# ScalarE instead of VectorE for the product of the first comparison with the large part of the gate

## The chip, the cores and the metric

The kernel runs on one core of one Trainium2 chip. The metric is the device time of one execution in microseconds; the figure before is the median of three runs. The engines are named as the profile names them: PE is TensorE, DVE is VectorE, ACT is ScalarE, POOL is GpSimd, SP issues the DMAs.

## The reference, cut to what matters

Two layers, each a mixer and a feed-forward block of retrieved experts (PEER), and then two more layers of another kind. The change lies in the feed-forward block of the first two layers alone. For each of 256 tokens and 8 heads it finds 16 experts out of 128 x 128, weighs them by a softmax and adds their outputs:

```
top_s, top_pos = lax.top_k(cand, PEER_TOPK)
eid = jnp.take_along_axis(cand_id, top_pos, axis=-1)
g = jax.nn.softmax(top_s, axis=-1)
ue = u_tab[eid]
ve = v_tab[eid]
act = jax.nn.gelu(jnp.einsum('pd,phkd->phk', xb, ue))
return jnp.einsum('phk,phkd->pd', g.astype(xb.dtype) * act, ve)
```

The expert number is i1 * 128 + i2. The kernel gathers nothing: it computes gelu(u . x) for all 16384 experts as a dense product, and makes a dense gate matrix with g where a token has chosen the expert and zero elsewhere.

## The kernel before, in words

`peer` (L764) works on 128 row blocks of 128 experts, in two phases. The **u phase** (L994 to L1013) is a loop over b, and each turn of it is called a body here. Body b issues, in this order:

1. `u_split(b + 2)`: the DMA of a block of the table, its rounded copy `hi` on ACT (L153) and the remainder `lo` on DVE (L81, in `tt`). So the two parts of block b are made two bodies ahead.
2. what the body before left in `later`.
3. a share of `tasks` (the top-16 search, in the first 54 bodies), or, in bodies 55 to 121, `group(b)`.
4. `u_block(b)`: 24 matmuls of block b into one bank `up` (L228 to L230), and the gelu on ACT: L971 in place for the P tokens whose gate already stands in row b, L974 into the row for the other tokens. The product of gate and gelu (DVE, `Wx<-up,Wx` or `Wy<-up,Wy`) goes to `later`.
5. what the body before left in `after`.

PE, DVE and ACT run this loop under `manual_schedule`, so each keeps the order in which the code issues its instructions.

A **group** makes the gate of 8 tokens for all experts. `g_onehots` compares a row of numbers with i2 (tile B) and with i1 (tile L), then multiplies L with the large half-precision part gH of the gate (tile A) and, in place, with the small part gL. Two bodies later `g_matmuls` makes 16 matmuls (L939), eight with A and then eight with L, into two banks `gg`, after the matmuls of that block. One body after that `g_store` puts the result away: DVE multiplies the rows whose gelu already stands there (`Wy<-gg,Wy`, `Wx<-gg,Wx`), ACT copies the rest (L952). There are 32 groups, in bodies 55, 56, 58, 60, 62, 64, 67, 69, 71, 73, 75, 78 and so on to 121: mostly every second body, and after every fifth or sixth group a distance of three bodies (67, 78, 89, 102 and 113 follow such a distance).

So the DVE order of a body with a group is lo(b+2), product of row b-1, B, L, A, L; the gg matmuls of group b come after block b+2, and its store is in body b+3.

The **v phase** (L1039 on) multiplies the finished rows with the second table. Before its sums can begin it needs the banks that the u phase held.

The other names: `i1T`, `i2T`, `gH`, `gL` are filled by `store` in `to_pairs` (L897 to L901), once for each half of the tokens.

Of the kernel before, what the change touches and what calls it, by code (L numbers as in the profile page):

```python
# [8 lines left out]
F32 = mybir.dt.float32  # L9
# [5 lines left out]
AF = mybir.ActivationFunctionType  # L15
ALU = mybir.AluOpType
# [4 lines left out]
S = 256  # L21
# [26 lines left out]
def kernel(ctx: ExitStack, tc: tile.TileContext, x, cols, ada_w, w_in, gm_wt, gm_vnorm, w_out,  # L48
# [3 lines left out]
    ve, se, pe, gp, sy = nc.vector, nc.scalar, nc.tensor, nc.gpsimd, nc.sync  # L52
# [24 lines left out]
    def two_banks(name):  # L77
        return psc["pool"].tile([128, 2, 512], F32, tag="c", name=name, bufs=2)

    def tt(out, a, b, op):  # L80
        return ve.tensor_tensor(out, a, b, op)  # L81

    def ts(out, a, s1, s2, op0, op1=None):
        if op1 is None:
            return ve.tensor_scalar(out, a, s1, None, op0)
        return ve.tensor_scalar(out, a, s1, s2, op0, op1)
# [452 lines left out]
    class Lead:  # L539
# [15 lines left out]
        def small(self, t, k0=0, k1=8):  # L555
            for k, wh, wl, g, d in self.parts(t):
                if k0 <= k < k1:
                    pe.matmul(d, lhsT=self.hT[1][:, k, t * 128:t * 128 + 128], rhs=wh[:, g * 512:g * 512 + 512],
                              start=False, stop=False, skip_group_check=True)
# [204 lines left out]
    def peer(l, hT, then):  # L764
        with ExitStack() as es:
            scr = es.enter_context(tc.tile_pool(name=f"pr{l}", bufs=1))
# [15 lines left out]
            i2T = scr.tile([128, S], F16, name="i2T")  # L782
            gH = scr.tile([128, S], F16, name="gH")
            gL = scr.tile([128, S], F16, name="gL")
            tasks = []
            tk = Scr(W, 20)
            st = {}
# [93 lines left out]
            def soft(t):  # L881
                s = st[t]
                e = s["e"]
                z = tk.tile([128, 8], F32, name="sm_z")
                ve.tensor_reduce(z, e, AX.X, ALU.add)
                ve.reciprocal(z, z)
                tt(e, e, z.rearrange("p (a b) -> p a b", b=1).to_broadcast([128, 8, 16]), ALU.mult)
                after.append(lambda: to_pairs(t))

            def to_pairs(t):  # L890
                s = st[t]
                ps = two_banks("tr")[:, 0, :]
                for n, src in enumerate((s["ii"][:, 0], s["ii"][:, 1], s["e"])):
                    pe.transpose(ps[:, n * 128:n * 128 + 128], src.rearrange("p a b -> p (a b)"), ident)
                c = slice(t * 128, t * 128 + 128)

                def store():  # L897
                    ve.tensor_copy(i1T[:, c], ps[:, 0:128])
                    ve.tensor_copy(i2T[:, c], ps[:, 128:256])
                    ts(gH[:, c], ps[:, 256:384], GSCALE, None, ALU.mult)  # L900
                    ve.scalar_tensor_tensor(gL[:, c], ps[:, 256:384], GSCALE, gH[:, c], ALU.mult, ALU.subtract)  # L901

                later.append(store)

# [13 lines left out]
            NG = 8  # L918

            def g_onehots(p0):  # L920

                shape = [128, NG // 2, 128, 2]
                A = scr.tile(shape, F16, name="A", tag="A", bufs=2)
                B = scr.tile(shape, F16, name="B", tag="B", bufs=2)
                L = scr.tile(shape, F16, name="L", tag="L", bufs=GL)
                it = iota2.rearrange("p (o i) q -> p o i q", o=1).to_broadcast(shape)
                tok = lambda a: a[:, p0:p0 + NG].rearrange("p (g o q) -> p g o q", o=1, q=2).to_broadcast(shape)
                tt(B, it, tok(i2T), ALU.is_equal)
                tt(L, it, tok(i1T), ALU.is_equal)
                tt(A, L, tok(gH), ALU.mult)  # L930
                tt(L, L, tok(gL), ALU.mult)
                return A, B, L

            def g_matmuls(p0, A, B, L):
                ps = two_banks("gg")
                for side in (A, L):
                    for n in range(NG):
                        a, q = divmod(n, 4)
                        pe.matmul(ps[:, a, q * 128:q * 128 + 128], lhsT=B[:, n // 2, :, n % 2], rhs=side[:, n // 2, :, n % 2],  # L939
                                  start=side is A and q == 0, stop=side is L, skip_group_check=True)  # L940
                return ps

            def g_store(p0, ps, nb):
                g3 = ps.rearrange("p g (q i) -> p (g q) i", q=4)
                for todo in (False, True):
                    for a, b0, b1 in ((Y, 0, NY), (W, NY, 128)):
                        wv, gv = a[:, :, p0:p0 + NG].rearrange("p i q -> p q i"), g3[:, :, b0:b1]
                        n = max(0, min(nb, b1) - b0)
                        if todo and n:
                            tt(wv[:, :, :n], gv[:, :, :n], wv[:, :, :n], ALU.mult)  # L950
                        if not todo and n < b1 - b0:
                            se.activation(wv[:, :, n:], gv[:, :, n:], AF.Copy)  # L952
# [4 lines left out]
            ready, after, later = [], [], []  # L957
# [18 lines left out]
            def group(b):  # L976
                p0 = st["groups"]
                st["groups"] += NG
                abl = g_onehots(p0)

                def matmuls():
                    banks = g_matmuls(p0, *abl)

                    def store():
                        g_store(p0, banks, st["block"])
                        st["stored"] += NG
                    later.append(store)
                after.append(lambda: after.append(matmuls))

            small_banks(True)  # L990
            for t in range(T):
# [2 lines left out]
            with tc.manual_schedule(engines={mybir.EngineType.PE, mybir.EngineType.DVE, mybir.EngineType.Activation}):  # L994
                for b in range(2):
                    u_split(b)
                for b in range(129):
                    st["block"] = b
                    u_split(b + 2)
                    now, later = later, []  # L1000
                    for f in now:
                        f()
                    if b == 128:
                        break
                    now, after = after, []
                    while tasks and spent < (b + 1) * total / TK:
                        spent += tasks[0][0]
                        tasks.pop(0)[1]()
                    if b > TK and st["groups"] < S and st["groups"] < (b + 1 - TK) * S / (GE - TK):
                        group(b)  # L1010
                    u_block(b)
                    for f in now:
                        f()  # L1013
# [616 lines left out]
    for l in range(2):  # L1630
        mixer(l, cur["hT"], then_norm(l, 4, "norm_ffn", 24, True))
        peer(l, cur["hT"], then_norm(1, 1, "norm_mix", 0, False, lambda: lead_half(w_in[1, :, 512:1024])) if l == 0 else then_even)
# [56 lines left out]
```

## Time and profile before

| what | us |
|---|---|
| median of three runs | 2326.93 (2321.4 to 2329.91) |
| the profiled execution, its own time | 2335.08 |
| its span | 2333.2 |
| PE busy | 2260.4 (97%) |
| DVE busy | 1762.8 (76%) |
| ACT busy | 1196.9 (51%) |
| granted TensorE clock, mean over the span | 0.993 |

A profile row of the timeline begins with the start in us from the start of the span and the duration in us. Durations overlap on one engine, since the next instruction starts before the last has written all of its result; what an instruction costs in a row of them is the distance from its start to the next start. The u phase with groups lies from 366 to 615 us in the first layer and from 1333 to 1582 us in the second.

### The profile page before, as it was taken

Reading aid. Unit: us, or ns where it says so; the run is one execution under the profiler, and the core shown is the slowest. Engines: PE = TensorE matmul, PEld = TensorE weight load, DVE = VectorE, ACT = ScalarE, POOL = GpSimd, SP = SyncE. Lnnn points to the kernel's source line nnn. Section 1 sums busy time; section 2 is a strip of 40 time slices with the busy share of each in tenths; the row PEclk is TensorE's granted clock in tenths of the full one; section 3 lists DMA queues with packets and bytes.
Section 4 is the critical chain, followed back from the end, with each engine's and each line's share of the span. In section 5 each row is a group of like instructions: output and inputs, shape, how many; then the busy total and the mean of one; then the engine's idle time right before and its main releaser. Section 6 shows DMA issues by size and latency. Waiting matters only on the chain.

```text
span 2333.2 us, 39116 instructions
## 1 busy us (share of the span) xinstructions
PE 2260.4 (97%) x14953; PEld 2021.3 (87%) x14953; DVE 1762.8 (76%) x3277; ACT 1196.9 (51%) x1925; POOL 13.3 (1%) x36
## 2 busy tenths in 40 slices
PE   5999999999999999999999999999999999999998
PEld 4889999999887787888899999998888877987796
DVE  7875999999867877666589899996555666577556
ACT  4645555554444444457455555544444554654454
POOL 0000000000000000000000000000000000000000
PEclk9999999999999999999999999999999999999999
DMA  8845555544568888644455554446656673443542
GB/s 321 280 139 159 185 181 172 156 153 154 172 207 286 299 298 278 210 140 127 138 158 186 183 158 153 157 142 196 190 187 187 203 226 97 133 136 116 173 153 82
DMA packets 122028, 424.11 MB, mean 182 GB/s; under 512 B 14433, under 2 KB 15841, under 8 KB 121842
## 3 DMA queue, kind: packets, MB, share of 16 engines
q1 hardware_dynamic: 121842, 421.63, 56.2%
q8 instruction: 117, 1.92, 0.3%
q14 instruction: 69, 0.57, 0.1%
HBM read 420.53 MB, written 1.05 MB: 181 GB/s over the span
## 4 chain that ended last, share of the span: by engine, by line
PE 78%; DVE 11%; DMA 6%; ACT 2%; issue 2%; SPq 0%; DVEq 0%; ACTq 0%
PE up L228 9%; PE up L229 8%; PE up L230 8%; PE op L1031 8%; PE op L1029 8%; PE op L1030 8%; DVE lo L81 4%; DMA Wx<-in_ada_w_dram 3%; PE pc L230 3%; PE pc L228 3%; PE pc L229 3%; DVE Wx L81 2%; PE gg L939 2%; DMA raw<-in_peer_v_dram 2%; PE op L238 2%
## 5 line engine op out<-in xcount | busy, mean ns | idle before, releaser
L81 DVE TENSOR_TENSOR lo<-raw,hi 128x1024 fp32r<-128x1024 f32 x686 | 835.4, 1222 | 323.1 <-ACT hi L153 322.2
L153 ACT ACTIVATE hi<-raw 128x1024 fp32r<-128x1024 f32 x686 | 720.0, 1052 | 266.6 <-PE pc L229 73.2
L230 PE MATMUL up<-hT_hi,lo 128*128 128x256 f32 x2048 | 581.7, 284 | 4.9 <-DVE lo L81 4.7
L228 PE MATMUL up<-hT_hi,hi 128*128 128x256 f32 x2048 | 585.8, 286 | 0.0
L229 PE MATMUL up<-hT_lo,hi 128*128 128x256 f32 x2048 | 580.0, 283 | 0.0
L230 PEld LDWEIGHTS up<-hT_hi,lo 128*128 128x128 f32 x2048 | 392.9, 192 | 8.4 <-DVE lo L81 8.4
L1031 PE MATMUL op<-hi,lo 128*128 128x512 f32 x976 | 388.3, 398 | 7.2 <-DVE lo L81 7.1
L229 PEld LDWEIGHTS up<-hT_lo,hi 128*128 128x128 f32 x2048 | 393.2, 192 | 0.0
L228 PEld LDWEIGHTS up<-hT_hi,hi 128*128 128x128 f32 x2048 | 392.9, 192 | 0.0
L1029 PE MATMUL op<-hi 128*128 128x512 f32 x976 | 387.9, 397 | 0.6 <-DVE Wx L81 0.5
L1030 PE MATMUL op<-lo,hi 128*128 128x512 f32 x976 | 387.2, 397 | 0.8 <-DVE lo L81 0.8
L1031 PEld LDWEIGHTS op<-hi,lo 128*128 128x128 f32 x976 | 184.2, 189 | 55.7 <-DVE lo L81 11.8
L1030 PEld LDWEIGHTS op<-lo,hi 128*128 128x128 f32 x976 | 184.1, 189 | 45.3 <-DVE lo L81 2.0
L1029 PEld LDWEIGHTS op<-hi 128*128 128x128 f32 x976 | 184.2, 189 | 44.7 <-DVE Wx L81 1.4
L228 PE MATMUL pc<-hT_hi,hi 128*128 128x256 f32 x568 | 161.1, 284 | 0.4 <-ACT hi L153 0.4
L229 PE MATMUL pc<-hT_lo,hi 128*128 128x256 f32 x568 | 160.9, 284 | 0.0
L230 PE MATMUL pc<-hT_hi,lo 128*128 128x256 f32 x568 | 160.7, 284 | 0.0
L971 ACT ACTIVATE up<-up 128x256 f32<-128x256 f32 (+31 forms) x140 | 37.7, 269 | 210.0 <-PE up L230 200.9
L153 ACT ACTIVATE hi<-Wy 128x256 fp32r<-128x256 f32 x120 | 50.1, 417 | 174.6 <-PE op L1030 174.6
L974 ACT ACTIVATE Wy<-up 128x256 f32<-128x256 f32 (+1 forms) x120 | 46.2, 385 | 166.2 <-PE up L230 166.0
L153 ACT ACTIVATE hi<-Wx 128x256 fp32r<-128x256 f32 x124 | 51.1, 414 | 126.5 <-PE op L1030 119.6
L228 PEld LDWEIGHTS pc<-hT_hi,hi 128*128 128x128 f32 x568 | 109.1, 192 | 1.4 <-ACT hi L153 1.3
(437 smaller groups left out, 3140.8 us busy)
## 6 DMA issues: line engine op xcount, KB each, us to landing
raw<-in_peer_ut_dram SPq DMA_DIRECT2D x256, 512.0 KB, 3.6
raw<-in_peer_v_dram SPq DMA_DIRECT2D x256, 512.0 KB, 4.3
Wx<-in_ada_w_dram SPq DMA_DIRECT2D x56, 512.0 KB, 5.6
raw<-in_even_w_dram SPq DMA_DIRECT2D x42, 512.0 KB, 3.6
raw<-in_w_in_dram SPq DMA_DIRECT2D x40, 512.0 KB, 4.8
raw<-in_peer_wq_dram SPq DMA_DIRECT2D x32, 512.0 KB, 4.1
raw<-in_odd_w_in_dram SPq DMA_DIRECT2D x32, 512.0 KB, 4.3
ada_raw<-in_ada_w_dram SPq DMA_DIRECT2D x30, 512.0 KB, 4.9
```

What stands on the lines that cost most here:

```text
L81: return ve.tensor_tensor(out, a, b, op)
L153: se.activation(hi, raw, AF.Copy)
L228: pe.matmul(dst, lhsT=wh[:, c0:c0 + 128], rhs=hh[:, k, :], start=first, stop=False, skip_group_check=True)
L229: pe.matmul(dst, lhsT=wh[:, c0:c0 + 128], rhs=hl[:, k, :], start=False, stop=False, skip_group_check=True)
L230: pe.matmul(dst, lhsT=wl[:, c0:c0 + 128], rhs=hh[:, k, :], start=False, stop=last, skip_group_check=True)
L238: pe.matmul(d, lhsT=a, rhs=wh[:, g * n:g * n + n], start=first, stop=False, **mk)
L939: pe.matmul(ps[:, a, q * 128:q * 128 + 128], lhsT=B[:, n // 2, :, n % 2], rhs=side[:, n // 2, :, n % 2], start=side is A and q == 0, stop= ...
L971: se.activation(ps[:, :P], ps[:, :P], AF.Gelu_apprx_tanh)
L974: se.activation(row(b)[:, P:], ps[:, P:256], AF.Gelu_apprx_tanh)
L1029: pe.matmul(d, lhsT=a, rhs=vh[:, s], start=first, stop=False, **mk)
L1030: pe.matmul(d, lhsT=a, rhs=vl[:, s], start=False, stop=False, **mk)
L1031: pe.matmul(d, lhsT=c, rhs=vh[:, s], start=False, stop=last, **mk)
```

## The change

DVE no longer makes A. In the body after the group, ACT makes it with eight `activation` copies, one for each token, each scaled by a per-partition number gF, which is a 32-bit copy of gH. The product with the small part overwrites L, so it has to wait for these eight; it moves to the end of that next body in DVE's order. The matmuls of the group stay where they were.

```
@@ peer
+            gF = scr.tile([128, S], F32, name="gF")
@@ to_pairs, store
+                    ve.tensor_copy(gF[:, c], gH[:, c])
@@ g_onehots
                 tt(B, it, tok(i2T), ALU.is_equal)
                 tt(L, it, tok(i1T), ALU.is_equal)
-                tt(A, L, tok(gH), ALU.mult)
-                tt(L, L, tok(gL), ALU.mult)
-                return A, B, L
+
+                def large():
+                    for n in range(NG):
+                        q = (slice(None), n // 2, slice(None), n % 2)
+                        se.activation(A[q], L[q], AF.Copy, scale=gF[:, p0 + n:p0 + n + 1])
+
+                def small():
+                    tt(L, L, tok(gL), ALU.mult)
+
+                return (A, B, L), large, small
@@ group
-                abl = g_onehots(p0)
+                abl, large, small = g_onehots(p0)
...
-                after.append(lambda: after.append(matmuls))
+
+                def rest():
+                    small()
+                    after.append(matmuls)
+
+                later.append(large)
+                after.append(rest)
```

In ACT's order body b+1 becomes: hi(b+3), the eight copies of group b, the store copy of group b-2 (where b-2 had a group), the gelu of block b+1. In DVE's order it becomes: lo(b+3), the product of row b, the store products of group b-2, the product of L with the small part.

## Rows read from the trace of the kernel before

**Rows 1.** The page, part 1: busy time of each engine over the span.

```profile
PE 2260.4 (97%) x14953; PEld 2021.3 (87%) x14953; DVE 1762.8 (76%) x3277; ACT 1196.9 (51%) x1925; POOL 13.3 (1%) x36
```

**Rows 2.** Stretches, first layer: PE, PEld, DVE, ACT, POOL busy; clock; DMA.

```profile
366.00:483.00 117.00, 117.00 (x1103) 116.32 (x1102) 108.35 (x161) 65.89 (x120) 0.00 (x0) 1.00 0.51 159
558.00:618.00 60.00, 57.44 (x497) 54.73 (x495) 58.78 (x77) 27.27 (x55) 0.00 (x0) 1.00 0.49 151
```

**Rows 3.** Timeline of PE: start, duration, instruction; group matmuls, start of v phase.

```profile
541.06 0.63 PE L939 MATMUL gg<-A,B 128*128 128x128 f16 x8
541.53 0.62 PE L939 MATMUL gg<-L,B 128*128 128x128 f16 x8
...
547.79 0.63 PE L939 MATMUL gg<-A,B 128*128 128x128 f16 x8
...
615.40 0.40 PE L1029 MATMUL op<-hi 128*128 128x512 f32 x1
...
1514.08 0.63 PE L939 MATMUL gg<-A,B 128*128 128x128 f16 x8
...
1581.81 0.40 PE L1029 MATMUL op<-hi 128*128 128x512 f32 x1
```

**Rows 4.** Timeline of DVE, bodies 106 and 107, from B of group 106.

```profile
543.90 0.67 DVE L81 TENSOR_TENSOR B<-iota,i2T 128x1024 f16<-128x1024 f16 x1
544.50 0.68 DVE L81 TENSOR_TENSOR L<-iota,i1T 128x1024 f16<-128x1024 f16 x1
545.22 0.69 DVE L81 TENSOR_TENSOR A<-L,gH 128x1024 f16<-128x1024 f16 x1
...
546.55 1.22 DVE L81 TENSOR_TENSOR lo<-raw,hi 128x1024 fp32r<-128x1024 f32 x1
547.69 0.34 DVE L81 TENSOR_TENSOR Wx<-up,Wx 128x184 f32<-128x184 f32 x1
547.95 1.25 DVE L81 TENSOR_TENSOR Wy<-gg,Wy 128x480 f32<-128x480 f32 x1
549.09 1.04 DVE L81 TENSOR_TENSOR Wx<-gg,Wx 128x376 f32<-128x376 f32 x1
550.01 1.23 DVE L81 TENSOR_TENSOR lo<-raw,hi 128x1024 fp32r<-128x1024 f32 x1
```

**Rows 5.** Timeline of ACT, gelu 106 to gelu 107; what ended an idle time in brackets.

```profile
541.25 0.31 ACT L971 ACTIVATE up<-up 128x184 f32<-128x184 f32 x1 [1.36 <-PE up L230]
...
541.72 1.06 ACT L153 ACTIVATE hi<-raw 128x1024 fp32r<-128x1024 f32 x1
542.67 0.47 ACT L952 ACTIVATE Wx<-gg 128x168 f32<-128x168 f32 x1
545.11 0.32 ACT L971 ACTIVATE up<-up 128x192 f32<-128x192 f32 x1 [1.97 <-PE up L230]
```

**Rows 6.** Timeline, the two store pieces whose width changes: ACT early, DVE late.

```profile
389.75 1.13 ACT L952 ACTIVATE Wx<-gg 128x536 f32<-128x536 f32 x1
...
604.47 1.27 DVE L81 TENSOR_TENSOR Wx<-gg,Wx 128x496 f32<-128x496 f32 x1
```

**Rows 7.** Timeline of ACT, and L741 by source: instructions nearest to the copies.

```profile
611.12 0.73 ACT L153 ACTIVATE hi<-Wx 128x256 fp32r<-128x256 f32 x2 [3.54 <-DVE Wx L81]
611.75 1.04 ACT L153 ACTIVATE hi<-raw 128x1024 fp32r<-128x1024 f32 x1
...
L741 ACT ACTIVATE xn<-X,rs_y x2: 1135/1142/1149, 12.3 to 13.4; 128x1024 f32<-128x1024 f32 x2
...
1944.03 2.15 ACT L396 ACTIVATE hT_hi<-tp,col 128x128 fp32r<-128x128 f32 x8
1946.02 0.68 ACT L204 ACTIVATE Wx<-Wx 128x512 f32<-128x512 f32 x1
...
1008.44 2.90 ACT L398 ACTIVATE hT_hi<-tp,mod,gain 128x128 fp32r<-128x128 f32 x8 [1.84 <-PE tp L223]
```

**Rows 8.** Timeline of DVE in `store` of `to_pairs`: a copy of 128 columns.

```profile
368.41 0.28 DVE L898 CAST i1T<-tr 128x128 f16<-128x128 f32 x1
```

## The prediction

> **What bounds the kernel now.** I read the shares of busy time first, then the stretches, then the timeline of each engine. Over the span PE is busy 97% of the time, DVE 76% and ACT 51% [rows 1]. That average says nothing of the u phase, so the stretches come next: up to 483 us PE has no hole at all and DVE is at 93%; from 558 to 618 us DVE has 58.8 of 60 us and PE's weight loads fall to 54.7 [rows 2]. So the phase is PE's until DVE falls behind, and DVE's at its end.
>
> How much that end costs is read from PE's timeline. With a group in every second body, two blocks and one group take 6.73 us (541.06 to 547.79) [rows 3]; one block and one group take 3.86 us, the distance of two gelus (541.25 to 545.11), since both wait for PE [rows 5]. So a block is 2.87 us and a group's matmuls are 0.99. The group matmuls at 547.79 are those of group 106, behind block 108. From there PE has 8 groups and 19 blocks to do, 7.9 + 54.5 = 62.4 us, and the v phase would begin at 610.2; it begins at 615.4 [rows 3]. PE has lost 5.2 us. In the second layer the same place is 1514.08 and the v phase begins at 1581.81, 67.7 us later: 5.3 lost [rows 3]. **Both layers together lose 10.4 us: that is all that a lighter DVE can give back**, 0.45% of the time.
>
> **What the change removes.** The product A costs DVE 0.7 us for each of 64 groups (0.69; L to A 0.72) [rows 4], 45 us of busy time. For two blocks and a group DVE has lo twice at 1.14, the row product m twice (0.26 at 184 columns), Wy at 1.14, Wx (x, 0.92 at 376 columns), B, L and the small part at 0.6 to 0.65 each: 5.4 + 2m + x = 6.8 us without A, against PE's 6.73; with A it was 7.5 [rows 4]. So after the change DVE alone would hold PE up only in the last groups, where x is about 1.2 (0.92 scaled by the row of 1.27 us [rows 6]) and m about 0.3, both estimates: 7.2 us, 0.45 too much.
>
> **What it adds on ACT.** Eight copies of 128 columns with a per-partition scale, from SBUF. No row has this form. Two copies of 256 columns from SBUF with no such scale follow each other at 0.315 us, since the next instruction starts 0.63 us behind the first [rows 7]; one of 1024 takes 0.95 from start to start [rows 5]; so a column costs 0.83 ns, and 128 columns 0.21. A scale per partition adds 0.08 (1.142 us for 1024 columns against 1.06) [rows 5, 7]. That is 0.29 us each, and p = 2.3 us for the eight. Bounds: eight of 128 columns from PSUM with one such operand took 1.99 us until the next instruction, eight with two took 2.90 [rows 7]. I take 2.3, since it is the sum for SBUF and lies between them; nothing shown excludes less for half precision, so 1.8 stays in a rival. ACT's total rises by 64 x 2.3 = 147 us to 58% of the span, far from full.
>
> The Trainium skill, page "ScalarE: Activation LUTs", section "What ACT_TABLE_LOAD costs", says that an ACTIVATE takes 186 ns plus 0.833 ns a column, 93 more for each per-partition operand, and that neighbours overlap by 93. By that the eight take 2.34 us, an estimate, and the sum below would be 2.4 us higher. The same page's "Rules for kernel authors" speaks against the change: it wants mul on VectorE and not on ScalarE. The row for DVE agrees (0.69 us against 2.3), but by engine time alone, with ACT half idle, the rule would cost nothing.
>
> **What it moves: a ring is closed.** The cost is in the order of the queues. DVE and ACT were loosely coupled: lo waits for hi, and nothing of a group went through ACT before its matmuls. Now the copies of group b wait for L(b) on DVE, and behind them in ACT's order stand the store copy of group b-2 (w), the gelus of block b+1 and hi(b+4); lo(b+4) waits for that hi, and behind lo(b+4) in DVE's order stand the product of row b+1, B(b+2) and L(b+2), for which the next eight copies wait. Once round, in row durations: p + w + gelus 0.47 (541.25 to 541.72) + hi 1.06 [rows 5] + lo 1.14 + m + B 0.60 + L until its reader starts 0.72 [rows 4] + two handovers = **p + w + m + 4.0 us, once for every group, against PE's 6.73.** w is 1.04 early (1.13 less the overlap of 0.09) [rows 6] and 0.38 at body 107 (0.47 less 0.09) [rows 5]; m goes from an estimated 0.1 to 0.3. With p = 2.3 the ring takes 7.4 us early, 7.1 in the middle and 6.9 late: longer than PE's two blocks everywhere. The idle time of ACT ahead of each gelu (1.36 and 1.97 us [rows 5]) does not help, since the copies don't come when ACT is idle, they come when L is ready.
>
> A late ring reaches PE through the small product. It stood in the group's own body; now it stands a body later, behind lo, m, Wy and x: 1.14 + m + 1.14 + x + 0.69 [rows 4] = 3.3 us early and 4.4 late behind L(b). PE's matmuls with L come 6.73 + 0.47 us (541.06 to 541.53, the half with A goes first [rows 3]) behind block b, so L(b) may be ready up to 3.9 us behind block b early, 2.8 late. Unhindered it is ready at 1.6 to 2.7. The first groups use up this room; from then on what the ring has too much is PE's loss.
>
> **The sum.** A cycle of five groups is 11 blocks, 5 x 0.99 + 11 x 2.87 = 36.5 us of PE. In it the ring goes round three times in full, once without w (behind a distance of three bodies the store has been done), and once with a further gelu, hi, Wy and x: 5p + 4w + 5m + x + 5 x 4.0 + 2.6. So PE loses **5p + 4w + 5m + x - 13.9** in each cycle. With w, m and x by linear steps between the rows above:
> - groups 67 to 75 (w 0.95, m 0.15, x 0.3): 11.5 + 3.8 + 0.75 + 0.3 - 13.9 = 2.4 us
> - 78 to 86 (0.75, 0.2, 0.45): 2.0
> - 89 to 99 (0.5, 0.24, 0.7; a sixth group adds p + w + m - 2.7 = 0.3): 1.8
> - 102 to 110 (0.35, 0.27, 0.9): 1.2
> - 113 to 121 (0.2, 0.3, 1.1): 1.0 by the ring, and 1.8 with DVE's own 0.3 more in three groups
> - the groups up to 64 only use up the room: 0.9; and the room shrinks by 1.1 from early to late, which PE pays too.
>
> Together 11.2 us a layer, 22.4 in both, in place of 10.4: **12 us more**. The profiled execution would take 2335.1 + 12 = 2347; it lies 8.2 us above the median of the runs, so the median goes from 2326.9 to 2339. The slope is 5 us of time for each cycle and us of p, 6 cycles and 2 layers, so 60: p = 2.0 gives about 2327 (late in the phase DVE's own excess remains, so the loss doesn't fall to nothing), p = 2.9 gives 2370.
>
> At nothing: the four copies into gF, about 0.3 us each like L898 [rows 8], lie in the task phase, where PE has no hole; uncovered they cost 1.1 us. No DMA moves in SP's order: a load may start when the lo three blocks before it has ended, three bodies ahead of the hi that needs it, and the lags above are shorter than that. No wait is gone that the matmuls with A would miss: A is ready 2.4 us behind L(b), long before 6.73.
>
> **Rivals.**
> - *The ring stays open* (not slower). If the copies take 1.8 us, the ring is 6.9 early and 6.4 late, the 3-body distances absorb the early excess, and only DVE's last groups cost: about 2.5 us a layer, so -5.4 us, 2321. For it: ACT's idle time, and half-precision operands, of which ACT has no row. Against it: every row with a per-partition operand. It decides from p of about 2.0 down, where the loss equals the 5.2 us of now. The floor, all 10.4 us back, is 2316.
> - *The copies are dearer.* At the 2.9 us of the row with two operands [rows 7] PE loses about 27 us a layer, +44: 2370. If each waits for the one ahead, as L974 does for L971 (its columns lie in the same bank), about 3.5 us, +79: 2406. Against it: L396 writes one tile in neighbouring pieces and overlaps [rows 7].
> - *It closes, but just so.* p of 2.0 to 2.15, or handovers that hide in the overlaps: 2326 to 2333, no change to be told.
>
> **How the numbers follow.** The forecast (p from 2.15 to 2.55, its own range 2333 to 2354) has 0.52, open 0.15, dearer 0.15, just so 0.18. The range reaches from 2320 to 2364: it leaves out the better half of the open ring and most of the dearer copies. What a measurement of this kernel can tell from no change is about 0.5%, 11.6 us, so 2315 and 2338.6. Faster by more than that is out of reach but for chance, since 10.4 us is all there is: 0.03. Slower has the dearer copies and the part of the forecast above p = 2.29, two thirds: 0.15 + 0.34 = 0.49. The rest is 0.48.
>
> **What would show it.** Right: the eight copies near 2.3 us from the first start to the next instruction's; idle time of PE ahead of L939, ended by DVE's product of L and gL, already in groups 62 to 86, where PE now has no hole; ACT's gelus starting behind the copies and not behind PE; the start of the v phase 6 us later relative to the first group. DVE busy should fall by 45 us and ACT's rise by more than 147, since durations overlap. Wrong: copies under 2 us, or no hole of PE ahead of 540 us. Then the ring is open and only the last groups count. A hole ended by `lo` in place of L would mean that the lag reaches PE through the blocks first, and that the room was taken too wide.

## The result, and the profile after

The changed kernel takes 2383.39 us (median of 6 runs, 2380.09 to 2385.1) beside 2328.3 us for the kernel before (6 runs on the same chip): ratio 1.0238, 95% interval 1.0225 to 1.0251. It is slower by 55 us, where 12 were forecast. The profiled execution of after took 2382.25 us with a span of 2380.5. Lines have moved: L939, L952, L971, L974 and L1029 of before are L948, L961, L980, L983 and L1044 of after, and the copies are L936.

The page of after, part 1 (busy time of each engine) and its group of the copies (busy, mean ns | idle before, releaser):

```profile
PE 2260.2 (95%) x14953; PEld 2018.6 (85%) x14953; DVE 1716.3 (72%) x3217; ACT 1340.5 (56%) x2437; POOL 13.9 (1%) x36
...
L936 ACT ACTIVATE A<-L,gF 128x128 f16<-128x128 f16 x512 | 159.5, 429 | 99.0 <-DVE L L81 99.0
```

Beside [rows 1] DVE has lost 46.5 us and ACT has gained 143.6; PE has the same work in a longer span. The stretches of after, the first being that of [rows 2], show where PE now stands still (columns as there):

```profile
366.00:483.00 117.00, 107.85 (x998) 106.03 (x997) 86.77 (x132) 91.61 (x225) 0.00 (x0) 1.00 0.47 145
558.00:640.00 82.00, 71.59 (x647) 70.25 (x647) 68.61 (x90) 53.89 (x143) 0.00 (x0) 0.98 0.45 136
```

In the early stretch, where PE had no hole, it now has 9 of 117 us, and DVE and ACT both have more idle time than that. No engine is full over the stretch, so something goes round. The granted clock (the third number from the end) is 1.00 early and 0.98 late: a lower clock accounts for some 1.6 us of the late stretch (0.02 of 82, an estimate). The waits of after from 366 to 660 us (who waited for whom: us in total, times, longest) name the links:

```profile
ACT A L936 <- DVE L L81: 48.8, 29, 2.8
DVE Wy L81 <- ACT Wx L961: 44.5, 25, 2.4
PEld L948 <- issue: 30.8, 24, 2.1
PE gg L948 <- DVE L L81: 27.8, 24, 2.0
DVE lo L81 <- ACT hi L153: 16.7, 23, 1.5
ACT up L980 <- PE up L230: 15.4, 9, 2.7
```

The second line was not foreseen: DVE's store product waits for ACT's store copy. Before, no wait of `Wy` stands in this list, and the longest is that of ACT's gelu for PE; now that is 15.4 us:

```profile
ACT up L971 <- PE up L230: 99.9, 64, 3.1
```

One turn of the ring, in ACT's timeline and then in DVE's (start, duration; idle time and what ended it in brackets):

```profile
390.68 2.49 ACT L936 ACTIVATE A<-L,gF 128x128 f16<-128x128 f16 x8 [1.48 <-DVE L L81]
393.04 1.10 ACT L961 ACTIVATE Wx<-gg 128x536 f32<-128x536 f32 x1
...
398.54 2.49 ACT L936 ACTIVATE A<-L,gF 128x128 f16<-128x128 f16 x8 [1.56 <-DVE L L81]
```

```profile
389.95 0.70 DVE L81 TENSOR_TENSOR L<-iota,i1T 128x1024 f16<-128x1024 f16 x1
390.55 1.23 DVE L81 TENSOR_TENSOR lo<-raw,hi 128x1024 fp32r<-128x1024 f32 x1
391.68 0.18 DVE L81 TENSOR_TENSOR Wx<-up,Wx 128x16 f32<-128x16 f32 x1
394.17 1.25 DVE L81 TENSOR_TENSOR Wy<-gg,Wy 128x480 f32<-128x480 f32 x1 [2.30 <-ACT Wx L961]
395.33 0.15 DVE L81 TENSOR_TENSOR Wx<-gg,Wx 128x8 f32<-128x8 f32 x1
395.40 0.67 DVE L81 TENSOR_TENSOR L<-L,gL 128x1024 f16<-128x1024 f16 x1
396.00 1.21 DVE L81 TENSOR_TENSOR lo<-raw,hi 128x1024 fp32r<-128x1024 f32 x1
397.14 0.16 DVE L81 TENSOR_TENSOR Wx<-up,Wx 128x24 f32<-128x24 f32 x1
397.23 0.67 DVE L81 TENSOR_TENSOR B<-iota,i2T 128x1024 f16<-128x1024 f16 x1
397.83 0.67 DVE L81 TENSOR_TENSOR L<-iota,i1T 128x1024 f16<-128x1024 f16 x1
```

From start to start, beginning with the copies at 390.68: copies 2.36, store copy 1.13, `Wy` with `Wx` 1.23, product with the small part 0.60, `lo` with the row product 1.23, B 0.60, L until the next copies 0.71. Together 7.86 us, the distance of the two groups of copies (390.68 to 398.54), against PE's 6.73 [rows 3]. Late in the phase the store copy is narrow and the `Wx` product wide, and the ring is longer still (ACT, then DVE):

```profile
608.00 2.49 ACT L936 ACTIVATE A<-L,gF 128x128 f16<-128x128 f16 x8 [2.70 <-DVE L L81]
610.36 0.29 ACT L961 ACTIVATE Wx<-gg 128x80 f32<-128x80 f32 x1
616.36 2.49 ACT L936 ACTIVATE A<-L,gF 128x128 f16<-128x128 f16 x8 [1.52 <-DVE L L81]
```

```profile
610.68 1.29 DVE L81 TENSOR_TENSOR Wy<-gg,Wy 128x480 f32<-128x480 f32 x1 [1.28 <-ACT Wx L961]
611.87 1.22 DVE L81 TENSOR_TENSOR Wx<-gg,Wx 128x464 f32<-128x464 f32 x1
```

That is 8.36 us. PE meets it at the half of the group's matmuls that reads L, already twenty microseconds into the stage, and the v phase begins late (PE's timeline):

```profile
394.53 0.63 PE L948 MATMUL gg<-A,B 128*128 128x128 f16 x8
396.13 0.62 PE L948 MATMUL gg<-L,B 128*128 128x128 f16 x8 [0.96 <-DVE L L81]
...
605.38 0.62 PE L948 MATMUL gg<-L,B 128*128 128x128 f16 x8 [2.01 <-DVE L L81]
...
642.36 0.40 PE L1044 MATMUL op<-hi 128*128 128x512 f32 x1
```

Between the groups lie 25 distances of two bodies; each too long by 1.13 (7.86) to 1.63 us (8.36) makes 28 to 41 us a layer, less what the room behind the distances of three bodies takes. Measured from the first matmul of the u phase to the first of the v phase, it lasts 405.6 us before (209.79 to 615.40) and 433.8 after (208.55 to 642.36): 28.2 more, and 28.2 again in the second layer. The two make 56.4 us, where the medians differ by 55. By the prediction's working, before lost 5.2 us of this phase, so PE's own work in it is an estimated 400.4, and after loses 33.4. The phase is the yardstick below (first layer of the profiled execution; the second layer repeats it within 0.3 us, but for 447.3 in e3_store_behind_gelu), since the stretch from one layer's v phase to the next layer's u phase varies by some us between profiles (560.7 before, 554.5 after).

### The profile page after: what moved, and what is told of

It reads as the page before. It is cut to its first block, busy times and chain, and to the rows that moved or that the text cites. A ratio compares the mean times of both kernels' runs of the same rounds, so it can differ in the third digit from the quotient of the medians.

```text
span 2380.5 us, 39314 instructions
## 1 busy us (share of the span) xinstructions
PE 2260.2 (95%) x14953; PEld 2018.6 (85%) x14953; DVE 1716.3 (72%) x3217; ACT 1340.5 (56%) x2437; POOL 13.9 (1%) x36
## 4 chain that ended last, share of the span: by engine, by line
PE 69%; DVE 11%; ACT 9%; DMA 5%; issue 5%; SPq 0%; ACTq 0%; DVEq 0%
PE op L1046 8%; PE op L1044 8%; PE op L1045 8%; PE up L228 6%; PE up L229 6%; PE up L230 6%; ACT A L936 5%; DVE lo L81 3%; DMA raw<-in_peer_v_dram 3%; PE pc L230 3%; PE pc L229 3%; PE pc L228 3%; DVE L L81 2%; ACT hi L153 1%; PE op L238 1%
## 5 line engine op out<-in xcount | busy, mean ns | idle before, releaser
L1044 PE MATMUL op<-hi 128*128 128x512 f32 x976 | 386.9, 396 | 0.0
L1044 PEld LDWEIGHTS op<-hi 128*128 128x128 f32 x976 | 183.4, 188 | 44.4 <-ACT hi L153 0.8
L936 ACT ACTIVATE A<-L,gF 128x128 f16<-128x128 f16 x512 | 159.5, 429 | 99.0 <-DVE L L81 99.0
L81 DVE TENSOR_TENSOR Wy<-gg,Wy 128x480 f32<-128x480 f32 (+1 forms) x64 | 80.8, 1263 | 89.0 <-ACT Wx L961 89.0
L983 ACT ACTIVATE Wy<-up 128x256 f32<-128x256 f32 (+1 forms) x120 | 46.1, 384 | 160.7 <-PE up L230 160.5
```

The source lines that it names most:

```text
L936: se.activation(A[q], L[q], AF.Copy, scale=gF[:, p0 + n:p0 + n + 1])
L983: se.activation(row(b)[:, P:], ps[:, P:256], AF.Gelu_apprx_tanh)
L1044: pe.matmul(d, lhsT=a, rhs=vh[:, s], start=first, stop=False, **mk)
```

## The experiments

All were timed beside the kernel before. The theory was that the place of the copies in ACT's order closes a ring through the store copy; the rivals were that the copies are too dear for ACT, that the moved product with the small part costs by itself, and that the prediction's own ring (through gelus and `hi`) did it.

| kernel | median | before beside it | ratio, 95% interval | u phase | lost by PE |
|---|---|---|---|---|---|
| before | | | | 405.6 | 5.2 |
| after | 2383.39 | 2328.3 | 1.0238 (1.0225 to 1.0251) | 433.8 | 33.4 |
| e1_store_first | 2321.39 | 2327.48 | 0.9972 (0.9959 to 0.9985) | 402.7 | 2.3 |
| e2_small_late | 2326.83 | 2327.48 | 0.9991 (0.9981 to 1.0) | 406.1 | 5.7 |
| e3_store_behind_gelu | 2410.16 | 2327.48 | 1.0348 (1.0323 to 1.0372) | 445.7 | 45.3 |
| e4_first_and_later | 2373.43 | 2327.48 | 1.0192 (1.0173 to 1.0212) | 428.5 | 28.1 |
| e5_other_source | 2345.32 | 2328.75 | 1.0074 (1.0052 to 1.0097) | 415.3 | 14.9 |
| e6_half_each | 2323.8 | 2328.75 | 0.9981 (0.9968 to 0.9994) | 404.0 | 3.6 |
| e7_all_apart | 2322.36 | 2328.75 | 0.9975 (0.9964 to 0.9986) | 401.9 | 1.5 |
| e8_apart_on_dve | 2322.2 | 2328.64 | 0.9972 (0.996 to 0.9984) | 402.6 | 2.2 |

### The same copies, behind the store copy

```diff
-                later.append(large)
+                copies.append(large)
...
-                    now, later = later, []
+                    now, later = later + copies, []
+                    copies.clear()
```

> The changed kernel with one edit: in the body after a group, ACT's store copy of the group before (L961) is issued ahead of the eight gate copies, not behind them; DVE's order is unchanged. Theory of the store wait: DVE's store products (Wy<-gg) wait for ACT's store copy, which in the changed kernel stands behind the eight copies; the ring is copies 2.36 + store copy w + Wy 1.13 + Wx x + small product 0.61 + lo 1.13 + m + B 0.60 + L 0.72 = 6.6 + w + x + m, 7.9 us early and 8.3 late. With the store copy ahead, Wy waits for nothing new, and only the ring through gelus and hi is left without w, about 6.4 + m us, under PE's 6.73. Then PE loses some 3 us a layer, late only: 2325 us (2320 to 2332), and DVE's idle time ahead of Wy, 44.5 us in the first layer's groups, is gone. Theory of the prediction, that the ring through gelus and hi is what costs and the store wait only a symptom of it: most of the loss stays, over 2360 us.

The whole loss is gone, and 6 us more: 2321.39. Every instruction of after is there; only the store copy has changed places with the eight copies. The waits from 366 to 650 us have no line for `Wy` any more, and those of PE are nearly nothing:

```profile
DVE lo L81 <- ACT hi L153: 35.9, 56, 1.5
...
ACT A L936 <- DVE L L81: 16.3, 19, 1.6
...
PE gg L948 <- DVE L L81: 1.2, 4, 0.7
```

PE's timeline is back at 6.73 us for two blocks and a group:

```profile
393.81 0.63 PE L948 MATMUL gg<-A,B 128*128 128x128 f16 x8
...
400.54 0.63 PE L948 MATMUL gg<-A,B 128*128 128x128 f16 x8
```

So the copies are not too dear for ACT; the order is what costs. The granted clock over the span is no rival: 0.986 in this profile, 0.989 in that of after. The prediction's own ring is open here too, by its own formula: the store copy now runs while the copies would wait for L, so w drops out, and p + m + 4.0 is 6.5 us early and 6.7 late with the measured 2.36, not over 6.73.

### The later product alone, A still on DVE

```diff
+                tt(A, L, tok(gH), ALU.mult)
...
-                later.append(large)
```

> The half of the change without ACT: DVE makes A in the group's own body as in the kernel before, but the product with the small part stands at the end of the next body as in the changed kernel. Theory of the store wait: the late small product costs only where DVE itself is too slow, since it has 5.4 + 2m + x + 0.7 us of work for two blocks and no longer any room for a lag: from the 78th block on 0.3, 1.2, 2.4 and 3.7 us a cycle, some 8 us a layer in place of 5.2, 2333 us (2328 to 2342). If the place of the small product is the cause, whoever makes A, the time is near that of the changed kernel, over 2360.

No change: 2326.83, below the range that was expected, since DVE's own excess had been put at some 8 us a layer and PE loses 5.7. The product with the small part may stand a body later at no price that can be told, and PE's wait for it is 4.1 us in 7 times where after has 27.8 in 24. That rival falls.

### The store copy still later

```diff
-                        g_store(p0, banks, st["block"])
+                        nb = st["block"]
+                        behind.append(lambda: g_store(p0, banks, nb))
...
+                    while behind:
+                        behind.pop(0)()
```

Here the store is issued behind the gelus of its body, with the copies still ahead of both.

> The changed kernel with the store of a group issued one step later in the same body: on ACT the store copy stands behind the gelus of that body, on DVE the order is unchanged. Theory of the store wait: the gelus, 0.47 us, come into the ring between the copies and the store products, so each of some 29 links a layer is 0.47 us longer: +27 us on the changed kernel, 2410 us (2400 to 2425). Theory of the ring through gelus and hi: ACT's chain from the copies to the next hi holds the same instructions in another order, so the time stays at 2383 (2378 to 2390).

27 us slower than after. The first two lines are waits from 376 to 650 us:

```profile
DVE Wy L81 <- ACT Wx L961: 63.6, 32, 2.8
ACT A L936 <- DVE L L81: 56.7, 24, 3.4
```

What is put between the copies and the store copy is added to the ring and comes out as time: the wait of `Wy` grows from 44.5 to 63.6 us, and the groups of copies, 7.86 us apart in after, are 8.35 apart here (391.28 to 399.63). The u phase is 11.9 us longer than that of after, where 25 distances of 0.47 make 11.8.

### Store first, and the matmuls one block later

```diff
-                    after.append(matmuls)
+                    after.append(lambda: after.append(matmuls))
```

This is added to the edit of the first experiment.

> The store copy ahead of the eight copies, and besides the matmuls of a group one block later, which gives the small product 2.87 us more before PE needs it. Theory of the store wait: no wait of PE is left but for what DVE's own work exceeds (36.2 us a cycle of 36.5 at the end), so PE gets back nearly all of the 10.4 us that the kernel before lost: 2319 us (2315 to 2324). If the copies cost through anything else, such as gelus and parts that come late, the time is above that of the kernel before, 2328.

A miss: 2373.43. The expectation saw only the room that PE's matmuls gain. But the store follows the matmuls, and a block later it falls into a body that has a group, so that `Wy` and `Wx` stand between `lo` and the comparisons in DVE's order. ACT's timeline, then DVE's, over one turn:

```profile
422.15 2.49 ACT L936 ACTIVATE A<-L,gF 128x128 f16<-128x128 f16 x8 [1.18 <-DVE L L81]
...
425.01 1.05 ACT L153 ACTIVATE hi<-raw 128x1024 fp32r<-128x1024 f32 x1
...
430.05 2.49 ACT L936 ACTIVATE A<-L,gF 128x128 f16<-128x128 f16 x8 [1.66 <-DVE L L81]
```

```profile
426.10 1.23 DVE L81 TENSOR_TENSOR lo<-raw,hi 128x1024 fp32r<-128x1024 f32 x1 [0.72 <-ACT hi L153]
...
427.36 1.26 DVE L81 TENSOR_TENSOR Wy<-gg,Wy 128x480 f32<-128x480 f32 x1
428.51 0.31 DVE L81 TENSOR_TENSOR Wx<-gg,Wx 128x88 f32<-128x88 f32 x1
428.72 0.70 DVE L81 TENSOR_TENSOR B<-iota,i2T 128x1024 f16<-128x1024 f16 x1
429.32 0.70 DVE L81 TENSOR_TENSOR L<-iota,i1T 128x1024 f16<-128x1024 f16 x1
```

Copies until the gelu 2.36, gelus 0.50, `hi` 1.09, `lo` with the row product 1.26, store products 1.36, B 0.60, L 0.73: 7.90 us. This is the prediction's ring, through gelus and `hi`, with the store products in it in place of the store copy. `Wy` no longer waits for ACT, and the time is lost all the same.

### A store copy that reads something else

```diff
-                            se.activation(wv[:, :, n:], gv[:, :, n:], AF.Copy)
+                            se.activation(wv[:, :, n:], row8[:, :, b0 + n:b1], AF.Copy)
```

`row8` is a constant row in SBUF (the tile `iota`), so this kernel leaves out the gate of the rows still to come; everything stands where it stands in after.

> The changed kernel with ACT's store copy (L961) reading a constant row of numbers in place of the banks gg, so the rows it fills hold other values (the gate of the rows still to come is left out); order, widths and engines stay. DVE's store product then waits for PE's group matmuls alone, no longer for the store copy behind the eight copies. Theory of the store wait: with that one wait gone, just the ring is left that the prediction described, p + w + m + 4.0 us, so the prediction's own sum must come out: PE loses some 11 to 13 us a layer, 2340 us (2332 to 2350). If the wait of Wy is not what made the difference between 2339 and 2383, the time stays near 2383. If the ring of the prediction is no ring at all, it falls to the 2321 of the run with the store copy ahead.

2345.32, 38 us less than after. ACT's timeline, then DVE's, at the place shown for after:

```profile
390.41 2.50 ACT L936 ACTIVATE A<-L,gF 128x128 f16<-128x128 f16 x8 [1.16 <-DVE L L81]
392.78 1.14 ACT L962 ACTIVATE Wx<-iota 128x536 f32<-128x536 f32 x1
...
397.92 2.50 ACT L936 ACTIVATE A<-L,gF 128x128 f16<-128x128 f16 x8 [1.17 <-DVE L L81]
```

```profile
391.51 1.27 DVE L81 TENSOR_TENSOR Wy<-gg,Wy 128x480 f32<-128x480 f32 x1
...
395.37 1.23 DVE L81 TENSOR_TENSOR lo<-raw,hi 128x1024 fp32r<-128x1024 f32 x1 [1.73 <-ACT hi L153]
```

`Wy` starts without a wait, though the copy takes as long and writes the same place: the wait was for the common source, the `gg` banks. What remains is the ring that was forecast, `lo` waiting for `hi` behind the copies: 7.51 us, where the prediction's sum gives 2.3 + 1.04 + 0.1 + 4.0 = 7.4, and 7.5 with the measured 2.36.

### Half of the product on each engine

```diff
+                tt(A[:, :2], L[:, :2], tok(gH)[:, :2], ALU.mult)
...
-                    for n in range(NG):
+                    for n in range(4, NG):
```

> The changed kernel with the gate product shared: DVE makes it for four tokens of a group in the group's body (0.36 us), ACT copies the other four in the next body, 1.18 us in place of 2.36. Theory of the store wait: every link of the ring is 1.18 us shorter, 5.4 + w + x + m = 6.6 us early, 6.9 in the middle, 7.1 late, about PE's 6.73; DVE has 0.36 more, 7.5 us for two blocks late. PE loses 3 to 4 us a layer, late: 2325 us (2319 to 2331). If the cost goes with the count of copies and not with a ring that has a threshold, half of the 55 us stays: 2355.

2323.8, as the ring says: with four copies it is some 1.2 us shorter, an estimated 6.7 us early and 7.2 late against PE's 6.73, though the order is that of after. PE loses 3.6 us a layer, where 3 to 4 were expected. PE's wait at the group's matmuls falls to 2.3 us in 5 times.

### Every part in a body of its own, with copies and without

In the first of two kernels the copies stand in body b+1, the small product in b+2 behind the comparisons, the matmuls follow block b+3, and the store is in body b+4 behind the comparisons and the small product. The second has the same order, with A made by DVE right behind them in the group's own body.

```diff
-                    later.append(store)
+                    due.setdefault((b + 4, 1), []).append(store)
...
-                later.append(large)
-                after.append(rest)
+                due.setdefault((b + 1, 2), []).append(large)
+                due.setdefault((b + 2, 0), []).append(small)
+                due.setdefault((b + 3, 3), []).append(matmuls)
```

The second kernel against the first:

```diff
-                        for n in range(NG):
-                            q = (slice(None), n // 2, slice(None), n % 2)
-                            se.activation(A[q], L[q], AF.Copy, scale=gF[:, p0 + n:p0 + n + 1])
+                    tt(A, L, tok(gH), ALU.mult)
...
-                due.setdefault((b + 1, 2), []).append(large)
+                due.setdefault((b, 0), []).append(large)
```

> Each step of a group in a body of its own: comparisons in body b, the eight ACT copies in b+1, the small product in b+2 behind the comparisons of the next group, the matmuls behind block b+3, the store in b+4 behind the comparisons and the small product. The run with matmuls one block later (2373 us) put the store products, 1.15 + x us, between lo and the comparisons, so the ring through gelus and hi became 6.4 + m + 1.15 + x = 7.9 us and more; here they stand behind L, and no store copy stands behind the eight copies. Theory of rings: both rings are open (6.4 + m against 6.73), the small product has some 2 us of room, and DVE's own work (36.2 us a cycle of 36.5 at the end) just fits: 2318 us (2314 to 2323), below the 2321 of the run with the store copy ahead. If the later matmuls themselves cost, the time is near 2373 again.

> The order with each step in a body of its own, but DVE makes the product with the large part again, right behind the comparisons; ACT makes no copies. It tells how much of the gain of that order is the order's and how much ACT's copies bring. Theory of rings: no ring goes through ACT here, so what is left is DVE's own work, which with A is 36.4 us a cycle from the 78th block, then 37.5, 38.9 and 40.2, against PE's 36.5: 7 us too much, less a room of 2 to 3 us: PE loses 4 to 5 us a layer, nearly the 5.2 of the kernel before: 2326 us (2322 to 2330). If the order alone brings the gain, the u phase is as short as with the copies on ACT, 401.9 us from its first matmul to the v phase, and the time 2322.

2322.36 and 2322.2. The first lies in its range, but not below the 2321.39 of the kernel with the store first, as was expected. I had expected the second near the kernel before, at 2326, since DVE has to do everything again; it came out at the 2322 that was named for the case that the order alone brings the gain. The stretch from 558 to 612 us, first with the copies, then without, then before (columns as in [rows 2]):

```profile
558.00:612.00 54.00, 53.12 (x482) 52.15 (x481) 51.73 (x68) 38.88 (x98) 0.00 (x0) 1.00 0.49 156
```

```profile
558.00:612.00 54.00, 52.46 (x481) 51.71 (x480) 53.97 (x72) 24.82 (x54) 0.00 (x0) 1.00 0.47 148
```

```profile
558.00:612.00 54.00, 51.44 (x457) 49.25 (x456) 53.59 (x69) 23.54 (x50) 0.00 (x0) 1.00 0.47 146
```

With A on DVE, DVE is full (53.97 of 54), as it is before, but PE is held up less: 52.46 against 51.44 us busy. PE's weight loads wait 0.5 us for `lo` in the stage, where before they wait 4.1. The order suggests why: DVE's lag now falls on the store products, which PE doesn't need at once; no run shows this by itself. Of the 3.7 us a layer that the first kernel wins over before, 3.0 come from the order and 0.7 from ACT's copies, by the u phases; the medians don't tell the two kernels apart.

## Why the prediction was wrong, and where it was right

**Right: the bound before.** PE's loss of 5.2 us a layer is all there was to win; the best order left 1.5.

**Right: the price of the copies.** 2.36 us from the copies to the next instruction, where 2.3 was taken, 0.295 each. The trace agrees with the estimate of 2.34 from the Trainium skill, "ScalarE: Activation LUTs", section "What ACT_TABLE_LOAD costs". It agrees in the distance only: a single copy lasts 429 ns in the profile, where the same figures give an estimate of 386, and neighbours overlap by 134 ns instead of 93.

**Right: the ring through gelus and `hi`, with its term mis-sized.** The kernel whose store copy reads elsewhere shows it alone: 7.51 us a turn where 7.4 was worked out, and 14.9 us lost a layer where the sum gave 11.2; its median is 16.6 above before, not 12. The copies, taken 0.06 us too cheap, make 1.8 of the missing 3.7 by the prediction's own slope (30 a layer); the rest stays open. In the changed kernel itself this ring is not the longest, so it isn't what set the time.

**Wrong: the step from L(b) to the small product.** The prediction counted what stands "behind lo, m, Wy and x" by durations alone, as if `Wy` waited for nothing, put the small product 3.3 us behind L(b) early, and so found room. In the turn shown for after it is 5.4 us behind (L over at 390.65, the small product at 396.07), and 2.30 of that is the wait of `Wy`. The prediction listed the store copy among what stands behind the copies on ACT, but followed only `hi` to the one who waits for it on DVE; the store copy was w in the sum and nothing else. `Wy`, which waits for it in DVE's order, closes a second ring, without gelus or `hi`: p + w + store products + small product + lo + m + B + L. The rows for this were there. In [rows 5] the store copy of body 107 is over at 542.67 + 0.47 = 543.14, and in [rows 4] the `Wy` of that body starts at 547.95: 4.8 us of room, so the wait never appeared in the trace of before. Early in the phase the room is smaller: the store copy of [rows 6] is over at 389.75 + 1.13 = 390.88, and its `Wy` starts 1.2 us later, again without a wait (DVE, before):

```profile
392.11 1.26 DVE L81 TENSOR_TENSOR Wy<-gg,Wy 128x480 f32<-128x480 f32 x1
```

A wait that is always met leaves no idle time and no line among the waits; only the instructions, the tiles they share and the order in the code tell of it. The copies, 2.36 us, came ahead of the store copy together with their own wait for L, and the room was gone.

That such a wait has to be there is what the Trainium skill, "PSUM — Partial Sum Buffer", section "PSUM bank collisions raise a hardware error", says: two engines may not be in the same bank (and the same quarter of the partitions) at once, even if both only read, and a semaphore has to keep them apart. The runs agree as far as they go: 25 waits, 44.5 us in one layer, where the copy reads the `gg` banks, and none where it reads SBUF. That the chip would go wrong without it, no run here shows. Had the prediction asked of each moved instruction which banks it or its neighbours share, it could have found the 7.9 us.

**The sum.** 33.4 us a layer in place of 11.2, and in place of the 5.2 of before: +56.4 in both layers, not +12. The range ended at 2364; it had some of the dearer copies in it, but no second ring.

**The rivals.** The open ring was put at 2321 with 2.5 us lost a layer. The first experiment measures 2321.39 and 2.3, with copies of full price: the order opens the ring, not cheap copies, so the likeness of the numbers is luck. The 2383.39 of the changed kernel lies between the 2370 and the 2406 that the prediction gave for dearer copies, by luck too: that rival falls by the 2.36 us. (By the prediction's own slope its 2.9 us make 2375, not 2370; nothing hangs on it.) "Just so" was tied to cheaper copies and falls with them.

**What would show it.** PE's idle time ended by L in the early groups, the gelus behind the copies, and DVE's busy time (46.5 less, 45 forecast) came as written. ACT's rose by 143.6 us and not by more than 147: busy time counts an overlap once. The 512 copies of 429 ns have 159.5 us of busy time between them, and part of that overlaps their neighbours. The v phase came 28.2 us later, not 6: this was the sign of another ring.

The prediction also put a rule of the Trainium skill against the change ("ScalarE: Activation LUTs", section "Rules for kernel authors"): multiplications belong on VectorE. By engine time the trace agrees, 0.69 us against 2.36 for the eight copies, but it doesn't decide the time here. In the same order, the product on ACT (2322.36) and on DVE (2322.2) cost the same, and the same copies in two orders differ by 62 us. What stays open: in `g_store` the copies are issued ahead of the products, and the other order, DVE's product first with ACT waiting, was not tried.

## What to carry to other kernels

When work moves to another engine, write down for every instruction behind it in that engine's order who reads or shares its tiles, above all who shares its PSUM banks, including waits that the trace of before never shows because they were always met. Then add up each closed path through two in-order queues from start to start, and compare it with what the bounding engine needs for the same turn. In this kernel it paid to issue the copies, which wait for DVE, behind the store copy, for which DVE waits: that was worth 62 us, and the choice of the engine nothing that the medians show.

## What the runs showed of the hardware

That two engines which only read the same banks stand one behind the other was not expected: up to 2.4 us of waiting for each group, 44.5 us in one layer. It is a wait that the program carries, gone when the copy reads something else; what the chip would do without it, no run shows. ACT's copy of 128 half-precision columns from SBUF with a scale per partition, of which before had no row, takes 429 ns, and eight in a row take 2.36 us until the next instruction.
